# Second RWKV layer: the inverses of the last head pairs' triangles made in steps between the scan's chunks, and y of both directions kept on its half of the partitions

## The chip, the cores and the metric

The kernel is one program on one core of a Trainium2 chip. The metric is the device time of one execution in microseconds (us). A core has five engines that run side by side and meet through semaphores: PE (TensorE, matrix products; its weight loads are shown as PEld), DVE (VectorE), ACT (ScalarE), POOL (GpSimd) and SP (SyncE, which here issues DMA transfers). Each takes its own instructions strictly in the order of the program; that order is fixed when the kernel is built.

## What is computed

The program is a whole model step; the change lies in its second RWKV-7 layer, whose core is a recurrence over the tokens, in two directions and 16 heads of 64:

```python
def rwkv7_scan(state0, r, decay, k_dir, v, kk, a, emit):
    ...
    def step(S, inp):
        w_t, k_t, v_t, kk_t, a_t = inp[:5]
        s_kk = jnp.einsum('nbhvk,nbhk->nbhv', S, kk_t)
        S = S * w_t[..., None, :] - s_kk[..., :, None] * (kk_t * a_t)[..., None, :] + v_t[..., :, None] * k_t[..., None, :]
        y_t = jnp.einsum('nbhvk,nbhk->nbhv', S, inp[5]) if emit else None
        return S, y_t

    s_final, ys = lax.scan(step, state0, seqs)
    ...
    ys = jnp.moveaxis(ys, 0, 2)
    y = ys[0] + jnp.flip(ys[1], axis=1)
    return s_final, y.reshape(bsz, length, RWKV_WIDTH)

def rwkv7_output(y, r, k_dir, v, z, r_k, ln_gain, ln_bias, w_out):
    ...
    yn = ((yh - mean) * lax.rsqrt(var + RWKV_LN_EPS)).reshape(y.shape) * ln_gain + ln_bias
    ...
    return (out * jax.nn.silu(z)) @ w_out
```

The kernel doesn't go token by token. It cuts the 768 tokens (256 of context, 512 latent) into 12 chunks of 64. Within a chunk the recurrence becomes matrix products, if the inverse of a 64x64 triangle is at hand for each chunk, head and direction. These triangle inverses are what the change moves.

## The kernel before

**Stages.** `_rwkv_features` (L651) goes over eight head pairs `hp`. For each it runs the projections, which stand as filler among the rest, and twice `direction` (one for each direction: the decays, `th` at L767, the scaled keys `bk` at L783 and L785, `ra` at L784 and L807/L809, and the triangles, which go to memory as `MD`). Then `_rwkv_scan` (L928) runs the chunks, `_rwkv_out` (L1078) normalises what they give, and the products with `w_out` follow.

**A triangle's inverse** is made in two steps. `_rwkv_diagonal` (L870) inverts the 32x32 blocks on the diagonal, 128 of them at a time, one on each partition. The 768 blocks of all pairs make six such lots, i = 0 to 5, which this text calls **blocks one to six**; lots 0 to 2 hold pairs 0 to 3, lots 3 to 5 pairs 4 to 7. Each is one load of `lm` from `MD`, two clears of `lw` on POOL, then 31 rounds of two DVE instructions, a product into `tm` (L881) and a sum into `lw` (L883), each needing the one before it; one ACT copy turns `lw` round, and the results are stored as `TL` and `TV`. `_rwkv_inverse` (L899) fills in the remaining 32x32 quarter for one pair: loads of `tt` and `v1`, then eight groups of 12 small matmuls (four into `pq`, four into `pw`, taken in turn, each evicted by ACT; the trace has two records for each matmul), then a store to `TD`, from where the scan loads it as `td`.

**When.** Blocks are made at the end of the turns hp = 1, 2, 3, 5, 6, 7; the inverse of a pair is started a turn later (`LAG`). Pairs 6 and 7 remain after the last turn; `inverses(9)` is returned as the generator `late`, which the scan advances once per chunk, with `issue_after` on the chunk's last matmul (L1052). The tiles `lm`, `lw` and `tm` lie in pool `rd`, which is closed before the scan's pools are opened on the same memory.

**The scan.** There are two chains, q = 0 for the even pairs and q = 1 for the odd ones, each of 4 pairs x 3 segments x 4 chunks, 48 chunks; chain 1 is two steps behind. `chunk` (L989) is issued with high priority. In it the matmuls L998 and L1000 give `x` (evicted at L1002 as `xs`), those of L1005 give `z` (evicted into `zv` at L1006 on ACT and L1007 on DVE), L1010 gives what is added to the state `S` (L1014, two DVE instructions), and the last ones give `y`. Both directions are worked at once: direction 0 on one half of the 128 partitions, direction 1 on the other. `prepare` (L953) makes ready the next segment while a segment runs: DMA loads of `kb`, `ar`, `td`, `zv` on SP's queue, the scaled keys `ks` on POOL (L974) with four transposes on PE (L976) and an eviction on ACT (L977), and the masked products `pgm` on PE (L983) and `aq` on DVE (L985). The first use of a set of buffers also clears the halves that are not loaded (L946, L948, L949, on POOL).

**y.** Before, `ys` is a tile of 64 partitions; each chunk's `py` (128x128) is evicted in two pieces of 64x128, direction 1's moved to partitions 0 to 63, by DVE for odd chunks (L1022) and ACT for even ones (L1024). `_rwkv_out` adds both directions in one DVE sum (L1102), the second read backwards.

**The order** of each engine's instructions isn't written out by hand. A scheduler sets it at build time from the code's order, priorities (`high_priority`) and `issue_after`.

## Time and profile before

| | |
|---|---|
| median of 3 runs | 4413.97 us (4413.07 to 4424.48) |
| profiled execution, its own time | 4423.36 us |
| its span | 4421.6 us |
| busy share of the span: PE, PEld, DVE, ACT, POOL | 91, 75, 62, 40, 34% |
| granted clock, mean | 0.944 |
| last feature stage of this layer | to about 2763 us |
| the scan's first `pgm` / first chunk | 2789.15 / 2842.11 us |
| the scan's last chunk | about 3254 us |

The profile is one execution, its times counted from the start of its span. The busy shares are means over many stages with different limits; for a change in one stage one reads that stretch. A row of the timeline gives in square brackets how long the engine was idle before the instruction, and which instruction or transfer ended the idle time ("<-DMA lm<-md": a transfer into `lm`). The granted clock is TensorE's as a share of its full 2.4 GHz.

### The profile page before, as it was taken

The page shows a single profiled execution, that of the slowest core. Times are in us where ns is not written, and L with a number is a line of the kernel's source. Part 1 is how long each engine was busy: PE and PEld are TensorE (multiplying, and loading weights), DVE is VectorE, ACT ScalarE, POOL GpSimd, SP SyncE. Part 2 cuts the span into 40 slices and gives each one's busy share as a digit, 9 for nine tenths or more (in the row PEclk, how much of TensorE's full clock was granted, in tenths as well). Part 3 has the DMA queues.
Part 4 walks back from the last instruction along what each step waited for, and adds up shares of the span by engine and source line. Part 5 has one row for each costly group of instructions (what it writes and reads, how often), then busy time and mean ns, then how long its engine had stood idle before and what let it go on. Part 6 is the DMA issues. An engine that isn't in the chain of part 4 may idle for free.

```text
span 4421.6 us, 67663 instructions
## 1 busy us (share of the span) xinstructions
PE 4026.0 (91%) x26396; PEld 3301.2 (75%) x26396; DVE 2741.8 (62%) x4409; ACT 1750.0 (40%) x3351; POOL 1513.2 (34%) x1046
## 2 busy tenths in 40 slices
PE   5888999988989999999988889588889999999999
PEld 3766767756766779888977777476668888887987
DVE  6455476776697874446676777555655466764443
ACT  4444454532232334224344445233323355543321
POOL 4332144453444441223335534335521222211221
PEclk7999999988999999999998989699989999999999
DMA  5123121235445563224534776654422311132232
GB/s 188 59 66 96 51 81 53 82 109 195 136 143 156 171 188 106 91 91 156 174 121 159 230 220 184 155 131 119 113 68 76 112 51 49 50 99 92 86 96 86
DMA packets 345551, 518.46 MB, mean 117 GB/s; under 512 B 114424, under 2 KB 217464, under 8 KB 343696
## 3 DMA queue, kind: packets, MB, share of 16 engines
q1 hardware_dynamic: 339040, 502.08, 37.4%
q10 hardware_dynamic: 6192, 12.06, 0.8%
q8 instruction: 208, 3.41, 0.3%
q14 instruction: 111, 0.91, 0.1%
HBM read 425.86 MB, written 88.19 MB: 116 GB/s over the span
## 4 chain that ended last, share of the span: by engine, by line
PE 58%; DVE 15%; DMA 7%; issue 4%; ACT 3%; POOL 2%; SPq 1%; DVEq 0%; ACTq 0%; POOLq 0%
DVE macc L127 3%; PE pz L102 3%; PE pz L103 3%; PE pz L101 3%; PE po L102 2%; DMA mraw<-mw 2%; PE po L101 2%; PE po L103 2%; PE pgm L983 2%; PE pu L101 2%; PE pu L103 2%; PE pu L102 2%; PE pv L101 2%; PE pv L102 2%; PE pv L103 2%
## 5 line engine op out<-in xcount | busy, mean ns | idle before, releaser
L93 POOL TENSOR_TENSOR wlo<-raw,whi 128x1024 fp32r<-128x1024 f32 (+2 forms) x254 | 570.8, 2248 | 1339.5 <-ACT whi L91 968.2
L91 ACT ACTIVATE whi<-raw 128x1024 fp32r<-128x1024 f32 (+3 forms) x399 | 383.4, 962 | 710.3 <-PE pz L102 132.2
L95 DVE TENSOR_TENSOR wlo<-raw,whi 128x1024 fp32r<-128x1024 f32 (+3 forms) x278 | 351.6, 1266 | 288.2 <-ACT whi L91 281.8
L127 DVE SCALAR_TENSOR_TENSOR macc<-mraw,conds,macc 128x1024 f32<-128x1024 f32 x168 | 268.8, 1615 | 37.7 <-DMA mraw<-mw 37.4
L103 PE MATMUL pu<-xh,wlo 128*128 128x512 f32 x608 | 243.6, 401 | 10.5 <-DVE wlo L95 6.6
L101 PE MATMUL pu<-xh,whi 128*128 128x512 f32 x608 | 241.2, 401 | 4.3 <-DVE fu L2054 3.0
L102 PE MATMUL pu<-xl,whi 128*128 128x512 f32 x608 | 242.3, 399 | 0.0
L89 DVE CAST whi<-raw 128x1024 fp32r<-128x1024 f32 (+2 forms) x133 | 98.1, 738 | 151.6 <-PE pz L102 46.6
L226 POOL TENSOR_TENSOR rsr<-rsv,mhalf 128x4 f32<-128x4 f32 (+3 forms) x56 | 77.8, 1391 | 276.1 <-DVE rsv L224 258.5
L102 PE MATMUL pz<-xl,whi 128*128 128x512 f32 x384 | 150.0, 391 | 0.0
L103 PEld LDWEIGHTS pu<-xh,wlo 128*128 128x128 f32 x608 | 116.2, 191 | 39.5 <-DVE wlo L95 7.5
L101 PE MATMUL pv<-whi,xh 128*128 128x256 f32 x512 | 139.0, 283 | 6.9 <-ACT whi L91 6.1
L983 PE MATMUL pgm<-ar,kb 128*128 128x256 f32 x384 | 122.1, 442 | 24.8 <-DMA ar<-fe 15.7
L102 PE MATMUL pv<-wlo,xh 128*128 128x256 f32 x512 | 142.4, 282 | 0.0
L101 PEld LDWEIGHTS pu<-xh,whi 128*128 128x128 f32 x608 | 116.4, 192 | 33.5 <-issue 4.1
L103 PE MATMUL pv<-whi,xl 128*128 128x256 f32 x512 | 140.3, 282 | 0.5 <-DVE xl L258 0.5
L102 PEld LDWEIGHTS pu<-xl,whi 128*128 128x128 f32 x608 | 116.4, 191 | 27.5 <-issue 0.3
L102 PE MATMUL po<-slo,whi 128*128 128x512 f32 (+1 forms) x384 | 136.1, 357 | 0.0
L103 PE MATMUL po<-shi,wlo 128*128 128x512 f32 (+1 forms) x384 | 135.4, 357 | 0.0
L101 PE MATMUL po<-shi,whi 128*128 128x512 f32 (+1 forms) x384 | 133.9, 364 | 0.5 <-ACT shi L111 0.5
L334 POOL TENSOR_TENSOR u<-u,z 128x512 f32<-128x512 f32 (+1 forms) x48 | 58.4, 1217 | 165.2 <-DVE z L325 165.2
L101 PE MATMUL pl<-xlh,whi 128*128 128x512 f32 x208 | 93.1, 451 | 13.2 <-DVE rp L1479 10.2
(747 smaller groups left out, 12948.7 us busy)
## 6 DMA issues: line engine op xcount, KB each, us to landing
mraw<-mw SPq DMA_DIRECT2D x128, 512.0 KB
raw<-G_wuz SPq DMA_DIRECT2D x96, 512.0 KB
raw<-G_wv SPq DMA_DIRECT2D x48, 512.0 KB
raw<-G_wout SPq DMA_DIRECT2D x48, 512.0 KB
raw<-F_w_up SPq DMA_DIRECT2D x44, 512.0 KB
raw<-R_w_in SPq DMA_DIRECT2D x70, 256.0 KB
raw<-S_w_xbc SPq DMA_DIRECT2D x24, 512.0 KB
fe<-ra SPq DMA_DIRECT2D x16, 768.0 KB
```

What stands on the lines that cost most here:

```text
L89: nc.vector.tensor_copy(hi, raw)
L91: nc.scalar.activation(hi, raw, AF.Copy)
L93: nc.gpsimd.tensor_tensor(lo, raw, hi.bitcast(F32), op=ALU.subtract)
L95: nc.vector.tensor_tensor(lo, raw, hi.bitcast(F32), op=ALU.subtract)
L101: nc.tensor.matmul(ps, a[0], b[0], start=start, stop=False)
L102: nc.tensor.matmul(ps, a[0], b[1], start=False, stop=False)
L103: return nc.tensor.matmul(ps, a[1], b[0], start=False, stop=stop)
L127: nc.vector.scalar_tensor_tensor(acc, raw, c[:, kt:kt + 1], acc, op0=ALU.mult, op1=ALU.add)
L226: nc.gpsimd.tensor_tensor(r, v, self.mhalf[:, :n], op=ALU.pow)
L334: nc.gpsimd.tensor_tensor(u, u, z, op=ALU.mult)
L983: nc.tensor.matmul(pgm[:, d], kb[:, i, d, :], ar[:, i, d], start=True, stop=True)
```

## The change

1. `_rwkv_diagonal` becomes a generator that yields after every fourth round and at its end.
2. In the features stage only blocks one to three are made, in turns 1 to 3, now in pool `ri` (`ipool`), which stays open through the scan. The inverses of pairs 0 to 3 are made there as before.
3. What the features return as `late` is now a chain: blocks four and five, the inverses of pairs 4 and 5, block six, two empty steps, the inverses of pairs 6 and 7. The scan advances it as before, once per chunk.
4. `ys` gets 128 partitions, and a chunk's `py` is evicted by one 128x128 instruction in place of two, by DVE for odd chunks and ACT for even ones. `_rwkv_out` first copies direction 1's half, backwards, to partitions 0 to 63 on ACT (28 copies, 20 of them of 64x512), then adds on DVE.

```diff
--- before.py
+++ after.py
@@ -827,7 +827,13 @@
         while done and done[0][0] <= hp:
             p = done.pop(0)[1]
-            yield from _rwkv_inverse(K, ipool, mts[p], TL[p], TV[p], tt, TD[p])
+            yield from inverse(p)
+
+    def inverse(p):
+        return _rwkv_inverse(K, ipool, mts[p], TL[p], TV[p], tt, TD[p])
+
+    def diagonal(i):
+        return _rwkv_diagonal(K, ipool, MD, TL, TV, i)
 
     mts, done = {}, []
     filler = fill()
@@ -854,12 +860,12 @@
             d1 = direction(hp, 1, k, r, nkk, l2)
             mts[hp], aks, _ = zip(d0, d1)
             bonus(hp, r, aks)
-        g = hp % 4
-        if g:
-            _rwkv_diagonal(K, rd, MD, TL, TV, hp // 4 * 3 + g - 1)
-            done.extend((hp + LAG, p) for p in ((hp - 1,) if g < 3 else (hp - 1, hp)))
+        if 0 < hp < 4:
+            for _ in diagonal(hp - 1):
+                pass
+            done.extend((hp + LAG, p) for p in ((hp - 1,) if hp < 3 else (hp - 1, hp)))
     c_f.close()
-    return inverses(9)
+    return chain(diagonal(3), diagonal(4), inverse(4), inverse(5), diagonal(5), (None,) * 2, inverse(6), inverse(7))
 
 
 NTEMP = 4
@@ -881,6 +887,8 @@
         nc.vector.tensor_tensor(tv, lm[:, 0:u, u:u + 1].to_broadcast([P, u, 32 - u]),
                                 lw[:, u:u + 1, u:32].to_broadcast([P, u, 32 - u]), op=ALU.mult)
         nc.vector.tensor_tensor(lw[:, 0:u, u:32], lw[:, 0:u, u:32], tv, op=ALU.add)
+        if u % 4 == 0:
+            yield
     lt = lm
     nc.scalar.activation(lt.rearrange("l t s -> l s t"), lw, AF.Copy)
 
@@ -894,6 +902,7 @@
             m = min(48 - u, n)
             nc.scalar.dma_start(TV[hp][u:u + m], lt[l0:l0 + m])
         u0 += n
+    yield
 
 
 def _rwkv_inverse(K, pool, mts, tl, tv, tt, td):
@@ -1017,11 +1026,10 @@
                 nc.tensor.matmul(py[ZR[d], h, :], ar[:, i, d, h, 0:64], S[:, d, :], start=True, stop=False)
             for d in range(2):
                 mm = nc.tensor.matmul(py[ZR[d], h, :], aq[:, d, h, 0:64], zv[:, i, d, h, :], start=False, stop=True)
-        for d in range(2):
-            if i % 2:
-                nc.vector.tensor_copy(y[:, i, d], py[ZR[d]])
-            else:
-                nc.scalar.activation(y[:, i, d], py[ZR[d]], AF.Copy)
+        if i % 2:
+            nc.vector.tensor_copy(y[:, i], py)
+        else:
+            nc.scalar.activation(y[:, i], py, AF.Copy)
         return mm, S2
 
 
@@ -1043,7 +1051,7 @@
                 if seg == 0:
                     states[q] = pool.tile([P, 2, CH], F32, tag="S", bufs=4, name=K.nm("S"))
                     nc.gpsimd.memset(states[q], 0.0)
-                ys[q] = pool.tile([64, 4, 2, 2, CH], F32, tag="ys", bufs=6, name=K.nm("ys"))
+                ys[q] = pool.tile([P, 4, 2, CH], F32, tag="ys", bufs=6, name=K.nm("ys"))
                 if n < 11:
                     ahead[q] = prepare(n + 1, q, *todo[q][n + 1], tiles)
             with K.tc.high_priority():
@@ -1098,8 +1107,8 @@
         nc.sync.dma_start(vo[:, 2 * j:2 * (j + n)].rearrange("p (i h) v -> p i (h v)", h=2),
                           VT[0][ts, hp * P:(hp + 1) * P].rearrange("(i p) f -> p i f", p=CH))
         nc.sync.dma_start(z[:, at[-1][1]], ZD[hp][:, ts])
-        back = y1[R, ::-1, 1]
-        nc.vector.tensor_tensor(y[:, js], y0[R, i:i + n, 0], back[:, i:i + n], op=ALU.add)
+        nc.scalar.activation(y[:, js], y1[V, ::-1][:, i:i + n], AF.Copy)
+        nc.vector.tensor_tensor(y[:, js], y0[R, i:i + n], y[:, js], op=ALU.add)
         j += n
     nc.vector.reduce_sum(mn, y3, axis=AX.X)
     nc.vector.tensor_scalar(mn, mn, 1.0 / CH, None, op0=ALU.mult)
```

Where the code stands says little of where the instructions go, since the scheduler orders them. Three places on DVE show it. The names are the buffers' with a number each; `lm`, `lw` and `tm` are those of a diagonal block. Line numbers after are 4 to 9 higher (L887 and L889 are L881 and L883 of before, L994 is L985, L1016 is L1007, L1023 is L1014).

DVE at the end of the features stage, before the change: the last two rounds of block four, then the last feature work of the last-but-one direction and of the last one (`th_24314`, `bk_24340`, `ra_24339`); `zo` is a projection's tile.

```order
L883 TENSOR_TENSOR lw_23275<-lw_23275,tm_23365 128x2x30
L881 TENSOR_TENSOR tm_23368<-lm_23273,lw_23275 128x31
L784 TENSOR_TENSOR ra_24149<-nkk_23454,e_4663_24135 128x12x64
L809 TENSOR_TENSOR ra_24149<-r_23456,e_4663_24135 128x12x64
L883 TENSOR_TENSOR lw_23275<-lw_23275,tm_23368 128x31
L783 SCALAR_TENSOR_TENSOR bk_24150<-th_24140,nkk_23454 128x12x64
L722 SCALAR_TENSOR_TENSOR zo_24056<-zo_24056,pc_24057 128x256
L785 SCALAR_TENSOR_TENSOR bk_24150<-bk_24150,th_24124 128x12x64
L722 SCALAR_TENSOR_TENSOR zo_24056<-zo_24056,pl_24058 128x512
L783 SCALAR_TENSOR_TENSOR bk_24340<-th_24330,nkk_23454 128x4x64
L767 SCALAR_TENSOR_TENSOR th_24314<-rmask,th_24314 128x768
L783 SCALAR_TENSOR_TENSOR bk_24340<-th_24330,nkk_23454 128x8x64
```

DVE at the same place after the change, from the row behind block four's last one: the same feature work, and in it the first rounds of block five (`lm_24722`); the last row is the beginning of the last direction's `bk`.

```order
L767 SCALAR_TENSOR_TENSOR th_23800<-rmask,th_23800 128x768
L784 TENSOR_TENSOR ra_23825<-nkk_23351,e_4588_23811 128x12x64
L809 TENSOR_TENSOR ra_23825<-r_23353,e_4588_23811 128x12x64
L783 SCALAR_TENSOR_TENSOR bk_23826<-th_23816,nkk_23351 128x12x64
L722 SCALAR_TENSOR_TENSOR zo_23732<-zo_23732,pc_23733 128x256
L785 SCALAR_TENSOR_TENSOR bk_23826<-bk_23826,th_23800 128x12x64
L722 SCALAR_TENSOR_TENSOR zo_23732<-zo_23732,pl_23734 128x512
L887 TENSOR_TENSOR tm_24727<-lm_24722,lw_24724 128x31
L889 TENSOR_TENSOR lw_24724<-lw_24724,tm_24727 128x31
L887 TENSOR_TENSOR tm_24730<-lm_24722,lw_24724 128x60
L889 TENSOR_TENSOR lw_24724<-lw_24724,tm_24730 128x30x2
L783 SCALAR_TENSOR_TENSOR bk_23898<-th_23888,nkk_23351 128x4x64
```

Block four's end has moved ahead of the last-but-one direction's `ra` and `bk`, and block five's beginning stands ahead of the last direction's `bk`, where before all of block five stood behind it.

DVE where the scan begins, before: the last round of block six, then the first products `aq` (the first chunks' operands), and the first chunk's `zv` and `S`.

```order
L881 TENSOR_TENSOR tm_24502<-lm_24407,lw_24409 128x31
L883 TENSOR_TENSOR lw_24409<-lw_24409,tm_24502 128x31
L985 TENSOR_TENSOR aq_24583<-pgm_24580,r_rmask 128x512
L985 TENSOR_TENSOR aq_24588<-pgm_24585,r_rmask 128x512
L985 TENSOR_TENSOR aq_24593<-pgm_24590,r_rmask 128x512
L985 TENSOR_TENSOR aq_24598<-pgm_24595,r_rmask 128x512
L1007 COPY zv_24544<-c_4765_24660 64x128
L1014 SCALAR_TENSOR_TENSOR S_24682<-S_24657,gam,c_4765_24660 128x64 x2
```

The same place after: the first four `aq` and the first chunk's `zv`, with rounds of block five around them.

```order
L994 TENSOR_TENSOR aq_24039<-pgm_24036,r_rmask 128x512
L889 TENSOR_TENSOR lw_24724<-lw_24724,tm_24990 128x12x20
L994 TENSOR_TENSOR aq_24044<-pgm_24041,r_rmask 128x512
L887 TENSOR_TENSOR tm_25044<-lm_24722,lw_24724 128x231
L889 TENSOR_TENSOR lw_24724<-lw_24724,tm_25044 128x11x21
L887 TENSOR_TENSOR tm_25047<-lm_24722,lw_24724 128x220
L994 TENSOR_TENSOR aq_24049<-pgm_24046,r_rmask 128x512
L889 TENSOR_TENSOR lw_24724<-lw_24724,tm_25047 128x10x22
L887 TENSOR_TENSOR tm_25050<-lm_24722,lw_24724 128x207
L994 TENSOR_TENSOR aq_24054<-pgm_24051,r_rmask 128x512
L889 TENSOR_TENSOR lw_24724<-lw_24724,tm_25050 128x9x23
L1016 COPY zv_24000<-c_4648_24116 64x128
```

Before, blocks five and six stand wholly ahead of the first `aq`. After, the first `aq` stands ahead of block five's last 11 rounds, and block six is not there.

DVE some chunks later, before: only `aq` of the next segments and the chunks' `zv` and `S`.

```order
L1007 COPY zv_24544<-c_4784_24786 64x128
L1014 SCALAR_TENSOR_TENSOR S_24808<-S_24738,gam,c_4784_24786 128x64 x2
L985 TENSOR_TENSOR aq_25182<-pgm_25179,r_rmask 128x512
L1007 COPY zv_24601<-c_4795_24848 64x128
L1007 COPY zv_24544<-c_4805_24918 64x128
L1014 SCALAR_TENSOR_TENSOR S_24870<-S_24845,gam,c_4795_24848 128x64 x2
```

After, the same kind of chunk work with rounds of block six (`lm_26337`) in it.

```order
L887 TENSOR_TENSOR tm_26404<-lm_26337,lw_26339 128x175
L1023 SCALAR_TENSOR_TENSOR S_24533<-S_24386,gam,c_4731_24511 128x64 x2
L994 TENSOR_TENSOR aq_24798<-pgm_24795,r_rmask 128x512
L889 TENSOR_TENSOR lw_26339<-lw_26339,tm_26404 128x25x7
L887 TENSOR_TENSOR tm_26407<-lm_26337,lw_26339 128x192
L889 TENSOR_TENSOR lw_26339<-lw_26339,tm_26407 128x24x8
L887 TENSOR_TENSOR tm_26455<-lm_26337,lw_26339 128x207
L1016 COPY zv_24057<-c_4740_24568 64x128
L889 TENSOR_TENSOR lw_26339<-lw_26339,tm_26455 128x23x9
L887 TENSOR_TENSOR tm_26458<-lm_26337,lw_26339 128x220
L889 TENSOR_TENSOR lw_26339<-lw_26339,tm_26458 128x22x10
L887 TENSOR_TENSOR tm_26461<-lm_26337,lw_26339 128x231
```

Block six's rounds now stand between the chunks' `zv`, `S` and the next segments' `aq`, some two to four instructions between two of the chunks' own. On PE, the groups of pairs 4 and 5, which stood ahead of the first chunk, now stand between chunks 18 and 42 of the 96, and those of pairs 6 and 7 between chunks 44 and 65.

## Rows read from the trace of the kernel before

**Rows 1.** Busy time by stretch: us, each engine, granted clock, DMA share, GB/s.
```profile
core 0: us, PE busy (x) PEld busy (x) DVE busy (x) ACT busy (x) POOL busy (x), PEclk, DMA share, GB/s
2477.00:2763.00 286.00, 257.34 (x2360) 214.62 (x2362) 230.18 (x383) 144.95 (x270) 120.72 (x110) 0.87 0.69 202
2763.00:2842.00 79.00, 33.49 (x481) 29.33 (x476) 53.94 (x136) 17.36 (x31) 18.49 (x24) 0.55 0.69 156
2842.00:2966.00 124.00, 113.73 (x1760) 91.90 (x1760) 55.11 (x149) 40.34 (x114) 45.28 (x50) 0.90 0.50 125
2966.00:3254.00 288.00, 247.30 (x3919) 195.56 (x3916) 179.02 (x487) 94.82 (x287) 129.33 (x125) 0.95 0.41 110
```

**Rows 2.** Timeline of the hole: start us, us, engine, line, operation [idle before].
```profile
2762.89 1.77 DVE L783 SCALAR_TENSOR_TENSOR bk<-th,nkk 128x256 f32<-128x256 f32 x1 [0.95 <-ACT th L754]
...
2772.27 0.21 DVE L881 TENSOR_TENSOR tm<-lm,lw 128x31 f32<-128x31 f32 x1 [1.66 <-DMA lm<-md]
...
2813.49 0.20 DVE L881 TENSOR_TENSOR tm<-lm,lw 128x31 f32<-128x31 f32 x1 [13.59 <-DMA lm<-md]
...
2841.36 1.29 DVE L985 TENSOR_TENSOR aq<-pgm,r_rmask 128x512 f32<-128x512 f32 x2 [4.46 <-DMA tv<-lm]
...
2849.34 0.47 DVE L1014 SCALAR_TENSOR_TENSOR S<-S,gam,c 128x64 f32<-128x64 f32 x2 [0.71 <-PE c L1010]
...
2784.06 1.93 POOL L946 MEMSET ar<- 64x1024 f32 x2 [8.65 <-DMA md<-mt]
...
2785.93 0.52 POOL L948 MEMSET zv<- 64x512 f32 x1
...
2841.40 2.04 POOL L974 TENSOR_TENSOR ks<-kb,gam 128x512 f32<-128x512 f32 x2 [32.31 <-DMA tv<-lm]
...
2789.15 2.07 PE L983 MATMUL pgm<-ar,kb 128*128 128x256 f32 x4
...
2842.11 0.48 PE L998 MATMUL c<-zv,aq 128*64 128x64 f32 x4 [14.85 <-DMA tt<-tl]
...
2847.14 0.66 PE L976 MATMUL pb<-ident,ks 128*128 128x128 f32 x4
...
2848.77 0.45 PE L1010 MATMUL c<-zv,bk 128*64 128x64 f32 x8 [0.58 <-DVE zv L1007]
...
2847.84 0.60 ACT L977 ACTIVATE bk<-pb 128x512 f32<-128x512 f32 x1 [0.30 <-PE pb L976]
```

**Rows 3.** Waits, 2780 to 2860 us: us in total, times, longest.
```profile
POOL ks L974 <- DMA tv<-lm: 32.3, 1, 32.3
```

**Rows 4.** Block four (its own DVE time, then all engines) and block six (all engines).
```profile
2703.00:2757.00 54.00, 31.07 (x62) 0.91 0.53 146
...
2703.00:2757.00 54.00, 50.43 (x516) 42.72 (x516) 50.41 (x86) 25.13 (x48) 23.97 (x21) 0.91 0.53 146
...
2813.00:2837.00 24.00, 10.38 (x168) 9.44 (x168) 21.25 (x62) 3.67 (x9) 0.00 (x0) 0.50 0.26 50
```

**Rows 5.** Inverse groups in the scan: tile pq, then tile pw.
```profile
2842.00:2966.00 124.00, 8.60 (x192) 7.05 (x192) 3.86 (x8) 0.90 0.50 125
...
2842.00:2966.00 124.00, 10.07 (x192) 8.02 (x192) 3.83 (x8) 0.90 0.50 125
```

**Rows 6.** Chunks by stretch, counted by their xs evictions on ACT (x).
```profile
2873.00:2966.00 93.00, 5.34 (x20) 0.93 0.47 116
2966.00:3254.00 288.00, 19.13 (x72) 0.95 0.41 110
```

**Rows 7.** Evictions of y, squares: ns min/median/max, first and last start; forms.
```profile
L1024 ACT ACTIVATE ys<-c x96: 254/273/276, 2849.7 to 3252.7; 64x128 f32<-64x128 f32 x96
...
L1108 ACT ACTIVATE ysq<-y x26: 416/617/631, 2885.5 to 3267.8; 64x512 f32<-64x512 f32 x20, 64x384 f32<-64x384 f32 x4, 64x256 f32<-64x256 f32 x2
```

**Rows 8.** Waits of PE in the scan, 3003 to 3253 us.
```profile
PE pgm L983 <- DMA ar<-fe: 9.8, 7, 2.9
```

**Rows 9.** A load of the inverses in the chain of waits: start us, us.
```profile
2918.90 5.43 DMA tt<-tl
```

## The prediction

> **What bounds the kernel now.** The shares of the whole span help little here, since the change touches one stage; I read that stage in this order. First the busy times by stretch [rows 1]. In the features stage (2477 to 2763 us) PE is busy for 257 of 286 us. From 2763 to 2842 it is busy for 33 of 79 us, at a granted clock of 0.55, that is about the lower of its two levels (1.2 and 2.4 GHz). In the scan (2842 to 3254) it is busy for 361 of 412 us. So there is a hole of 79 us between features and scan.
>
> Then the timeline of that hole [rows 2]. The last feature work that the scan's operands need, the `bk` of the last direction, starts at 2762.89. The scan's buffers are cleared from 2784.06, its first `pgm` matmul runs at 2789.15. But the first chunk's matmul comes at 2842.11. In between DVE runs the fifth block of diagonal inverses, 62 instructions from 2772.27; then it waits 13.59 us for the load of the sixth block's `lm`, and starts that at 2813.49; block five had ended at 2799.90. The first `aq` comes at 2841.36, after an idle 4.46, so block six ended at 2836.90. The waits name what follows [rows 3]: POOL's first `ks` waits 32.3 us for the transfer `tv<-lm`, the last reader of `lm`. `lm` and `lw` lie in pool `rd`, which closes before the scan's pools open on the same memory, so the scan can't write `ks` or `aq` before the last diagonal block has left it; DVE's order says the same, with all of block six ahead of the first `aq`.
>
> In the scan itself the waits of PE are short: in 250 us the longest entry is 9.8 us, for a load of `ar` [rows 8]. PE is the bound there, so what is added to PE counts nearly in full.
>
> **The change part by part.** *Start of the scan.* Blocks four to six now lie in `ri`, which stays open, so the memory wait of 32.3 us goes. The order shows that blocks four and five stay where they were; block five now begins earlier, its first four instructions ahead of `bk` (L783) of the last direction, and its tail lies between the scan's first `aq`; block six moves behind chunk 3. What is late next? Two things. (a) Block five's first instruction waits for `lm`, in DVE's order now ahead of L783. Today L783 starts at 2762.89 and `lm` is there for the instruction at 2772.27 [rows 2], after a wait for that very transfer: if `lm` comes no earlier, the last feature work slips by 9.4 us; if it is there in time, by nothing. The store of `MD` that it reads is issued by the last-but-one direction, whose work moves up a little behind block four's earlier end (the first place of DVE's order), so I take 5. Twelve of block five's instructions now stand ahead of L785, each between 0.21 us (the first, [rows 2]) and 0.34 (the mean of block six, 21.25/62, [rows 4]): 3 us. Slip: 8 us, between 3 and 12.4. (b) POOL's clears: from 2784.06 on there are now three pairs of `ar` (1.93 us a pair) and nine of `zv` and `td` (0.52 each) ahead of `ks`: 10.5 us. So `ks` starts at 2784.06 + 8 + 10.5 = 2802.6; then one `ks` 1.02, the transposes about 0.7, their eviction 0.6, and the chunk's `S` matmuls 0.45: the first `S` update starts at about 2806, where today it starts at 2849.34 [rows 2]. **Start: 43 us earlier** (39 to 48 by the slip; 30 if a memory wait of the new layout, which no row shows, holds it further). PE's clock gives nothing: it falls in a hole of 40 us as it did in one of 79.
>
> *Inverses of pairs 4 and 5.* They cost nothing today: their 16 groups of small matmuls lie in the hole. In the scan the price is to be seen from pairs 6 and 7, which run there already. Two bounds: the 16 groups have 8.60 + 10.07 = 18.7 us of PE there [rows 5]; and the 20 chunks from 2873 to 2966, with 15 of the groups, take 93 us, where the 72 chunks after them take 288, or 4.0 each [rows 6]: 93 - 80 = 13 us, 14 for 16 groups. **+16.5 us** (14 to 18.7), between the two since neither row is nearer.
>
> *Block six in the scan.* Alone it takes 21.25 us, and POOL is then at 0.00; block four takes 31.07 us with POOL busy for 23.97 of 54 [rows 4]. In the scan POOL is busy for 129 of 288 us [rows 1], much as there, so 31 us is the size. DVE has room (179 of 288 us busy [rows 1]), and spread over some 18 chunks the block adds 1.7 us of DVE to each. It costs only where a block instruction stands ahead of `zv` or `S` when that is ready. 0 if always hidden, 31 if never. Each chunk has two such places; a wait of half an instruction of 0.5 us (31/62) at each gives 18 x 2 x 0.25 = 9, less a little that PE hides: **+7 us**, nearer to 0 since PE, not DVE, is the bound.
>
> The Trainium skill (GPSIMD Engine Reference, section 1, Specifications) says that GpSimd's SBUF interfaces are shared with VectorE, with contention for DVE instructions that take two inputs from SBUF. A block's instructions are of that kind, so by this rule moving block six beside a busy POOL is a loss in itself; the trace agrees in size, 21.25 us beside an idle POOL and 31.07 beside a busy one, but block four also ran with more DMA and PE work beside it. Without the rule the block would cost 18 x 2 x 0.17 = 6 in place of 9, and the sum would be 2 us lower.
>
> *SP.* The two inverses bring their loads (`tt`, `v`) and a store (`td`) between the segments' loads on SP's in-order queue. A `tt` takes 5.43 us [rows 9], and I estimate the same for the store of the same tile. Behind them stand `ar`, `zv` and `td` loads of the next segment, for which PE waits. In the stretch that has two inverses today PE lost little to it, so **+2 us** (0 to 22, below).
>
> *y.* 96 evictions of 64x128 on each of ACT and DVE (273 ns on ACT [rows 7], about as much on DVE) become 48 of 128x128 on each, at the price of `xs`, which has that size: 19.13/72 = 0.27 us [rows 6]. That is 13 us less on each, none of it on PE. 28 copies on ACT are new, most of 64x512, at the 0.617 us of the square of that size [rows 7]: 16 us. All of it lies beside PE; on the path only at the end, where the last sums wait for one copy more: **+0.5 us**.
>
> Sum: -43 + 16.5 + 7 + 2 + 0.5 = **-17 us**. The profiled execution took 4423.36 us (span 4421.6), 9.4 above the median of 4413.97; of its own time that gives 4406, and of the median **4397 us**.
>
> **Rivals.**
> 1. *Everything hides.* `lm` is in time (start -48), inverses at 14, block six in DVE's idle time, y's lighter evictions pay for the rest: -34, **4380 us**. For it: DVE idles for 109 of 288 us in the scan [rows 1]. Against: the slip.
> 2. *DVE takes the bound over from PE* while block six runs, each of its instructions in the way of a chunk's `zv` or `S`: +31 instead of 7, sum +7, **4421 us**, no change. For it: in the windows of blocks four and six DVE is busy for 50.41 of 54 and 21.25 of 24 us, so a block leaves little room there [rows 4]. Against: one chunk in five only.
> 3. *SP becomes late.* At each of the four inverses a store and a load (2 x 5.43 = 10.9 us) hold the next segment's loads; four times is 44: -43 + 18.7 + 7 + 44 = +27, **4441 us**, slower. It decides from the point where `ar` lands behind the `pgm` that reads it; PE waits for it already, 9.8 us in 7 places [rows 8], so there is no slack. Against: two inverses in the scan today show no such hold.
> 4. *The start doesn't move as far*: a wait on memory or `lm` leaves 15 of the 43 us: -15 + 26 = +11, **4425 us**.
>
> **How the numbers follow.** Forecast 0.50 (4397, its own range 4386 to 4408), rival 1 0.17, rival 2 0.16, rival 3 0.10, rival 4 0.07. 0.3% is 13 us, about what a measurement of this kernel can tell from no change. Faster by more than that (below 4401): all of rival 1 and 0.7 of the forecast, 0.52. Within: the rest of the forecast, rival 2 and half of rival 4, 0.34. Slower: rival 3 and the rest, 0.14. The range holds the forecast and rivals 1, 2 and most of 4: 4374 to 4428.
>
> **What would show it.** The first `S` update near 2806 us, POOL's `ks` without the 32 us wait: start right. If DVE waits 9 us or more for `lm` ahead of L783, the slip was too small. 32 inverse groups in the scan at about 1.1 us each, the scan some 26 us longer from its first chunk to its last. Block six with 30 us of DVE; PE waits for `zv` and `S` of under 10 us in its stretch. More than 20 us of PE waits for `ar` or `td` would be rival 3. The forecast is wrong if the first chunk is still behind 2830, or the scan grows by more than 40 us.

## The result: 0.988 of the time before, three times the forecast gain

The changed kernel takes 4363.75 us (median of 4 runs, 4357.2 to 4369.79) where the kernel before takes 4415.93 beside it: a ratio of 0.9878, 95% interval 0.9863 to 0.9894, or -52 us. The direction of the forecast was right. Its size, -17 us, was not: the time lies below the range of 4374 to 4428. A second set of runs of the changed kernel gave 0.9866 (0.9851 to 0.9881).

In the profiled executions the span goes from 4421.6 to 4363.5 us. I cut it at three marks of the trace: the start of the last `bk` row (L783 on DVE), the first and the last eviction `xs` of the 96 chunks (on ACT). From the last `bk` to the first `xs`, the hole, it is 81.0 us before (2766.25 to 2847.26) and 30.2 after (2764.63 to 2794.84). From the first to the last `xs`, the scan, it is 406.2 before and 403.8 after. So -50.8 us came from the hole and -2.4 from the scan, which has 16 more groups of inverse matmuls and block six in it; the remaining -4.9 lies ahead of these marks (-1.6) and behind them (-3.3). These are two single executions, 58.1 us apart, where the medians are 52 apart.

The busy times by stretch of the changed kernel, to be read against [rows 1] (us, each engine, granted clock, DMA share, GB/s):

```profile
2477.00:2763.00 286.00, 253.96 (x2370) 212.74 (x2368) 231.24 (x383) 147.97 (x275) 121.62 (x112) 0.89 0.72 207
2763.00:2795.00 32.00, 12.93 (x105) 10.05 (x106) 28.82 (x54) 3.98 (x8) 19.73 (x27) 0.57 0.75 192
2795.00:2915.00 120.00, 108.91 (x1684) 86.48 (x1684) 90.75 (x239) 43.33 (x112) 51.14 (x54) 0.97 0.53 143
2915.00:3199.00 284.00, 257.34 (x4348) 208.98 (x4346) 162.12 (x430) 102.96 (x284) 122.22 (x117) 0.95 0.48 123
```

The features stage is as it was. The stretch in which PE is mostly idle has shrunk from 79 to 32 us, and DVE is now busy in it for 28.82 of 32 us, mostly with block five. PE's share in what follows has risen: 257.34 of 284 us where it was 247.30 of 288.

The timeline of the changed kernel in the hole, against [rows 2] (start us, us, engine, line, operation, idle before):

```profile
2762.42 1.04 DVE L887 TENSOR_TENSOR tm<-lm,lw 128x31 f32<-128x31 f32 x1 [2.05 <-DMA lm<-md]
...
2764.13 0.42 DVE L783 SCALAR_TENSOR_TENSOR bk<-th,nkk 128x256 f32<-128x256 f32 x1
...
2775.08 0.95 DVE L785 SCALAR_TENSOR_TENSOR bk<-bk,th 128x768 f32<-128x768 f32 x1
...
2781.97 3.89 POOL L955 MEMSET ar<- 64x1024 f32 x4
...
2787.32 4.20 PE L992 MATMUL pgm<-ar,kb 128*128 128x256 f32 x8 [5.67 <-DMA ar<-fe]
...
2790.70 0.69 DVE L994 TENSOR_TENSOR aq<-pgm,r_rmask 128x512 f32<-128x512 f32 x1 [2.02 <-PE pgm L992]
...
2792.20 1.03 POOL L983 TENSOR_TENSOR ks<-kb,gam 128x512 f32<-128x512 f32 x1
...
2801.32 0.47 DVE L1023 SCALAR_TENSOR_TENSOR S<-S,gam,c 128x64 f32<-128x64 f32 x2
```

Block five finds its `lm` at 2762.42, after 2.05 us of waiting, and the last direction's `bk` starts at 2764.13 (before: 2762.89). The last step of that `bk`, L785 at 2775.08, has twelve instructions of block five ahead of it. In the kernel before it is this row:

```profile
2769.13 1.48 DVE L785 SCALAR_TENSOR_TENSOR bk<-bk,th 128x768 f32<-128x768 f32 x1
```

So by L785 the feature work slips by 6 us, near the 8 that I had taken. But the scan's start does not slip with it: POOL's clears begin at 2781.97, where before they began at 2784.06 and I had them 8 us later. POOL's first `ks` runs between them at 2792.20 with no wait, and the first `aq` waits for PE's `pgm`, not for memory. The first `S` comes at 2801.32; I had it at 2806, and before it was at 2849.34.

The inverse groups in the scan (tile `pq`, then `pw`; PE, PEld and ACT), block six's own DVE time and all engines beside it, and the longest wait of PE in the scan (us, times, longest), in the changed kernel and then in the kernel before:

```profile
2795.00:3199.00 404.00, 17.15 (x384) 14.09 (x384) 7.70 (x16) 0.96 0.49 129
...
2795.00:3199.00 404.00, 19.34 (x384) 14.92 (x384) 7.61 (x16) 0.96 0.49 129
...
2824.00:2876.00 52.00, 26.95 (x62) 1.00 0.42 115
...
2824.00:2876.00 52.00, 45.48 (x747) 35.80 (x747) 49.42 (x134) 16.44 (x48) 18.44 (x18) 1.00 0.42 115
...
PE pgm L992 <- DMA ar<-fe: 10.0, 8, 2.4
...
PE pgm L983 <- DMA ar<-fe: 15.7, 12, 2.9
```

The 32 groups take 17.15 + 19.34 = 36.5 us of PE, 1.14 each, as forecast (1.1). Block six takes 26.95 us of DVE beside a POOL that is busy for 18.44 of 52 us, between the 21.25 and 31.07 of [rows 4]. SP is not late: PE waits 10.0 us for `ar` in the whole scan, where before it waited 15.7. All the work is there, at the size expected, and yet the scan is no longer. That is what the experiments had to explain.

### The profile page after: what moved, and what is told of

Read it like the earlier page. It is cut to its first block, busy times and chain, and to the rows that moved or that the text cites. A ratio compares the mean times of both kernels' runs of the same rounds, so it can differ in the third digit from the quotient of the medians.

```text
span 4363.5 us, 67568 instructions
## 1 busy us (share of the span) xinstructions
PE 4007.8 (92%) x26396; PEld 3288.7 (75%) x26396; DVE 2739.3 (63%) x4361; ACT 1751.1 (40%) x3331; POOL 1507.5 (35%) x1046
## 5 line engine op out<-in xcount | busy, mean ns | idle before, releaser
L127 DVE SCALAR_TENSOR_TENSOR macc<-mraw,conds,macc 128x1024 f32<-128x1024 f32 x168 | 272.0, 1634 | 36.8 <-DMA mraw<-mw 36.5
L102 PEld LDWEIGHTS pu<-xl,whi 128*128 128x128 f32 x608 | 116.0, 191 | 29.1 <-DVE xl L258 1.8
L992 PE MATMUL pgm<-ar,kb 128*128 128x256 f32 x384 | 116.8, 427 | 18.9 <-DMA ar<-fe 15.7
```

The lines of the kernel that those rows point to most:

```text
L102: nc.tensor.matmul(ps, a[0], b[1], start=False, stop=False)
L127: nc.vector.scalar_tensor_tensor(acc, raw, c[:, kt:kt + 1], acc, op0=ALU.mult, op1=ALU.add)
L992: nc.tensor.matmul(pgm[:, d], kb[:, i, d, :], ar[:, i, d], start=True, stop=True)
```

## The experiments

Two theories stood at the beginning. **A:** the start of the scan gave the whole gain, and the work added to the scan hides in time in which the engines wait. **B:** the added work costs the 24 us of the prediction, and the lighter evictions of y gave them back. All ratios below are to the kernel before, run on the same chip beside them, with their 95% interval. "Hole" and "scan" are the two lengths defined above, in the one profiled execution of each, and "clock" is the granted clock from the first to the last `xs`.

| kernel | ratio (interval) | hole | scan | clock |
|---|---|---|---|---|
| before | 1 | 81.0 | 406.2 | 0.94 |
| changed | 0.9878 (0.9863 to 0.9894) | 30.2 | 403.8 | 0.96 |
| changed, again | 0.9866 (0.9851 to 0.9881) | 29.5 | 409.1 | 0.95 |
| y_only | 0.9906 (0.9889 to 0.9922) | 33.7 | 409.9 | 0.94 |
| y_and_pool | 0.9905 (0.9890 to 0.9920) | 35.3 | 409.8 | 0.93 |
| y_padded | 0.9960 (0.9948 to 0.9973) | 82.7 | 379.7 | 0.98 |
| y_padded_two | 0.9966 (0.9954 to 0.9978) | 82.9 | 392.2 | 0.95 |
| ys_three | 0.9956 (0.9944 to 0.9969) | 33.9 | 433.4 | 0.92 |
| before_swap | 0.9971 (0.9960 to 0.9983) | 82.4 | 393.3 | 0.95 |
| before_zv | 0.9971 (0.9960 to 0.9981) | 82.6 | 387.9 | 0.96 |
| no_inv45 | 0.9872 (0.9856 to 0.9887) | 31.6 | 396.0 | 0.95 |
| no_inv4567 | 0.9830 (0.9816 to 0.9843) | 29.1 | 383.5 | 0.96 |
| no_block6 | 0.9895 (0.9876 to 0.9914) | 29.0 | 421.7 | 0.91 |
| block6_small | 0.9905 (0.9887 to 0.9922) | 29.1 | 422.3 | 0.92 |
| after_two | 0.9913 (0.9898 to 0.9927) | 29.3 | 418.2 | 0.95 |
| td_on_act | 0.9897 (0.9881 to 0.9913) | 29.4 | 407.9 | 0.95 |
| after_swap | 0.9895 (0.9881 to 0.9908) | 29.3 | 418.2 | 0.94 |
| after_zv | 0.9882 (0.9866 to 0.9897) | 30.3 | 413.3 | 0.93 |

### What freed the start

First one part of the change alone, y in its new form, in the kernel before:

```diff
-        for d in range(2):
-            if i % 2:
-                nc.vector.tensor_copy(y[:, i, d], py[ZR[d]])
...
+        if i % 2:
+            nc.vector.tensor_copy(y[:, i], py)
...
-                ys[q] = pool.tile([64, 4, 2, 2, CH], F32, tag="ys", bufs=6, name=K.nm("ys"))
+                ys[q] = pool.tile([P, 4, 2, CH], F32, tag="ys", bufs=6, name=K.nm("ys"))
```

> The kernel before with the y change alone (one 128x128 eviction per chunk, the ACT copy ahead of the sum); blocks and inverses as before. Theory A (the start of the scan gave the whole gain, and the work added to the scan hid in engines' idle time): within 4 us of before, the scan 406 us from its first to its last chunk as before. Rival B (the added work cost the 24 us that the prediction has, and the lighter evictions of y shorten every chunk and gave them back): 15 to 25 us faster than before, with the scan 15 to 25 us shorter.

It gave 0.9906, -41 us, most of the whole gain. Neither theory had that: A had no difference, and B a shorter scan, but the scan is 409.9 us long. It is the hole that is shorter, 33.7 us. The blocks still lie in pool `rd` in this kernel. So the new y alone is enough to free the start, without the move of the blocks to `ri`. The last `bk` (DVE) and the first `xs` (ACT) in this kernel's timeline:

```profile
2764.91 0.66 DVE L783 SCALAR_TENSOR_TENSOR bk<-th,nkk 128x512 f32<-128x512 f32 x1
...
2798.61 0.28 ACT L1002 ACTIVATE xs<-c 128x128 f32<-128x128 f32 x1 [5.79 <-DMA td<-tt]
```

Much of the late work then runs among the chunks although no call was moved. Block six begins at 2820.73 (first row) and ends at 2859.85, and 12 of the 16 `pq` evictions on ACT, so 24 of the 32 inverse groups, come behind 2799 (second row):

```profile
2820.73 0.20 DVE L881 TENSOR_TENSOR tm<-lm,lw 128x31 f32<-128x31 f32 x1
...
2799.00:3209.00 410.00, 12.36 (x288) 10.36 (x288) 5.79 (x12) 0.94 0.50 125
```

Then the pool was changed as well, `_rwkv_diagonal(K, ipool, ...)` in place of `rd`, with all calls where they were:

> The kernel before with the y change and all six diagonal blocks in the pool that stays open, nothing moved in the code: DVE's order comes out as in the changed kernel (the first aq inside block five, block six among the chunks), but the inverses of pairs 4 and 5 stay ahead of the first chunk on PE. Theory A: if the memory wait alone held the start, this gets most of the 52 us, 4365 to 4375. Rival (PE's order holds the start too, since the first chunk stands behind groups that need block five, which ends near 2809, and their loads): the first chunk near 2825 to 2830, only 15 to 25 us faster than before, near 4395.

0.9905, as with y alone; with the new y in place the pool adds nothing. The pool without the new y was not run, so whether it would free the start by itself is not shown. The rival missed too: the hole is 35.3 us. Only pair 4's groups run in it (PE's last of them starts at 2778.46); pair 5's come from 2811.05 on, among the first chunks.

An old `ys` tile takes 4 KB on each of its partitions, the new one 2 KB, and there are six: 12 KB. Whether this memory is the cause was asked from both sides. The new form, with the tile padded to its old size:

```diff
-                ys[q] = pool.tile([P, 4, 2, CH], F32, tag="ys", bufs=6, name=K.nm("ys"))
+                ys[q] = pool.tile([P, 8, 2, CH], F32, tag="ys", bufs=6, name=K.nm("ys"))[:, 0:4]
```

> The kernel before with the y change, but the tile of ys padded to its former 4 KB per partition, so that the scan's pools lie where they lay before. Theory M (the y change works by the 12 KB that it frees: the scan's ks and aq no longer lie on the memory of the last diagonal blocks): the start of the scan goes back, 80 us between the last bk and the first chunk, POOL's ks waits over 30 us again, and the time is within 6 us of before. Rival E (the lighter evictions and the sum's form gave the 42 us): as fast as with the y change alone, 4375 to 4382.

And the old form, with three buffers (`bufs=6` to `bufs=3`) in the kernel before:

> The kernel before with 3 buffers of ys in place of 6 and nothing else: the same 12 KB are free, y as before. Theory M: the first chunk comes some 34 us after the last bk, not 81, and the time is 35 to 45 us under before, less what waits for a free ys cost later. Rival E: no faster than before, or slower by those waits.

The hole says memory in both: 82.7 us with the padding, 33.9 with three buffers. The padded kernel's longest wait of POOL from 2780 to 2860 us (us, times, longest) is that of [rows 3]; then the last `bk` and the first `xs` with three buffers:

```profile
POOL ks L974 <- DMA tv<-lm: 32.8, 1, 32.8
```

```profile
2770.80 0.66 DVE L783 SCALAR_TENSOR_TENSOR bk<-th,nkk 128x512 f32<-128x512 f32 x1
...
2804.75 0.28 ACT L1002 ACTIVATE xs<-c 128x128 f32<-128x128 f32 x1 [6.05 <-DMA ar<-fe]
```

So this much is shown: with 12 KB less in `ys`, whatever the form of y, the wait of 32 us for the memory of the last diagonal block goes. The total time did not do what theory M said, though. The padded kernel is at 0.9960, not at 1; and with three buffers the scan takes 433.4 us, so 0.9956 and not 0.991. The padded kernel's scan is 26 us shorter than that of the kernel before. The waits for a free `ys` that were expected with three buffers are only 1.9 us of that long scan (us, times, longest); the rest of its length is not explained:

```profile
ACT ys L1024 <- DVE y L1102: 1.9, 3, 1.3
```

### What the moved work costs

The changed kernel with parts of the late work left out: the groups of pairs 4 and 5, those of all four pairs (in `_rwkv_inverse`, the matmuls and evictions are skipped and the yields stay), and block six:

```diff
     for u in range(31, 0, -1):
+        if i == 5:
+            if u % 4 == 0:
+                yield
+            continue
```

> The changed kernel without the 16 groups of small matmuls of pairs 4 and 5 and their evictions (left out; their loads and stores stay). Theory A (they hide in PE's idle time): 0 to 6 us faster than the changed kernel, 4358 to 4364. Rival B (the prediction's price): 14 to 19 us faster, 4345 to 4350.

> The changed kernel without the 32 groups of small matmuls of pairs 4 to 7 and their evictions (left out; loads and stores stay). Theory A (they hide in PE's idle time in the scan): at most 10 us faster than the changed kernel. Rival B (each counts in full, as the prediction has it): 28 to 37 us faster.

> The changed kernel without the 62 DVE instructions of block six (left out; its load, clears, copy and stores stay). Theory A: 0 to 3 us faster than the changed kernel, 4361 to 4364. Rival B (the prediction's price): 7 us faster, 4357; if DVE is in the way wherever it stands, up to 25.

Without 16 groups nothing is gained that can be measured (0.9872); without 32 it is 0.9830 against 0.9878 and 0.9866, that is 16 to 21 us, where the groups have 36.5 us of PE. More than A's 10 us came out, and less than B's 28. Against the changed kernel's two other orders (below) it would be 23 and 29 us, so between a fifth and somewhat over half of the groups' time hides. The scans of the kernel before, of the changed kernel and of the one without the 32 groups, first to last `xs`:

```profile
2847.26:3253.49 406.23, 355.70 (x5636) 283.50 (x5636) 231.77 (x629) 134.28 (x398) 169.49 (x166) 0.94 0.44 114
```

```profile
2794.84:3198.63 403.79, 366.04 (x6029) 295.44 (x6030) 252.71 (x668) 146.18 (x395) 173.53 (x171) 0.96 0.49 129
```

```profile
2797.07:3180.58 383.51, 328.02 (x5260) 263.20 (x5260) 251.35 (x668) 132.37 (x363) 175.70 (x172) 0.96 0.53 134
```

PE sits idle for 403.79 - 366.04 = 37.8 us in the changed kernel and for 383.51 - 328.02 = 55.5 without the groups; before, it was 406.23 - 355.70 = 50.5. Without them PE is busy for 38.0 us less, but the scan is only 20.3 us shorter: the groups fill idle time.

Block six showed no price. Without its 62 instructions the kernel is not faster but, if anything, slower, with one of the longest scans:

```profile
2790.40:3212.06 421.66, 376.44 (x6030) 305.09 (x6030) 228.11 (x609) 148.45 (x397) 175.05 (x173) 0.91 0.48 124
```

PE has no less and no more to do than in the changed kernel, but is busy for 376.44 us, at a granted clock of 0.91. The scan's length times its clock is 421.66 x 0.91 = 384 us here and 403.79 x 0.96 = 388 in the changed kernel, so by this estimate the clock makes the whole difference between the two scans; why it is lower here is not shown. The four runs of this kernel, 4363.94, 4370.97, 4379.1 and 4379.52 us, stand in the order of their granted clock over the whole program, 0.953, 0.951, 0.946 and 0.946. To keep the instructions in place I then cut them to one element each in place of leaving them out:

> The changed kernel with block six's 62 DVE instructions cut to one element each (the rest of their work left out), so that the number and the dependences of the instructions stay. DVE has some 22 us less to do among the first 20 chunks. The prediction's price: 5 to 9 us faster than the changed kernel. If block six hides: within 4 us. If, as without block six, the time goes up, the scan's time hangs more on TensorE's granted clock (0.91 over the scan without block six, 0.95 and 0.96 in the changed kernel) than on DVE's work, and the clock in this scan says so.

0.9905 and a scan of 422.3 us at 0.92: the same. So the scan does not get shorter with less work on DVE. A price of a few us, such as the 7 of the prediction, is not excluded by that, since both edits can change the scheduler's order as well, and an order alone can make such a difference, as follows.

### The order and the clock

That left the 16 us which the new form of y gives when it frees no memory. Two evictions per chunk in place of one, each on its own half, were tried in the padded kernel and in the changed one:

```diff
-        if i % 2:
-            nc.vector.tensor_copy(y[:, i], py)
+        for d in range(2):
+            if i % 2:
+                nc.vector.tensor_copy(y[ZR[d], i], py[ZR[d]])
```

> As y_padded, but each chunk's y evicted by two instructions of 64x128 again (each on its own half of the partitions). Theory C (the second eviction stands on ACT or DVE ahead of the next chunk's xs, zv or S and lengthens every chunk by some 0.2 us): 14 to 20 us slower than y_padded, so about as before (0.998 to 1.002 of it), the scan over 400 us where y_padded has 380. Rival F (the tile on 128 partitions and the new form of the sum gave the gain, not the number of evictions): as y_padded, 0.996.

> The changed kernel with two evictions of 64x128 per chunk, each on its own half: memory, blocks and inverses as in the changed kernel. Theory C: 12 to 20 us slower than the changed kernel, 0.990 to 0.992 of before. Rival F: as the changed kernel, 0.987.

The two contradict each other: no difference in the padded kernel (0.9966 against 0.9960), 15 us in the changed one (0.9913). What the scheduler does can explain it, since another eviction gives it other instructions to order. So the last four kernels keep the work and change the order: in the kernel before and in the changed one, the engines of y's evictions are changed over (`i % 2 == 0`), or those of the two `zv` evictions.

> The kernel before with the engines of y's evictions changed over (DVE takes the even chunks, ACT the odd ones): the same work, memory and counts, but the scheduler puts some 550 of DVE's instructions elsewhere. Theory O (the scan's time hangs on the order that the scheduler happens to find, by TensorE's short waits and the clock that falls after them): anywhere from 15 us faster to 15 us slower than before. Theory Y (the new form of y saves 15 us by itself): within 5 us of before.

> The kernel before with the two zv evictions of a chunk changed over between ACT and DVE: the same work, another order (some 450 of DVE's instructions elsewhere). Theory O: anywhere from 15 us faster to 15 us slower than before. Theory Y: within 5 us of before.

> The changed kernel with the engines of y's evictions changed over: the same work, another order (some 800 of DVE's instructions elsewhere). Theory O: up to 15 us from the changed kernel, and slower rather than faster, as the other variants of it were. Theory Y: within 5 us of it.

> The changed kernel with the two zv evictions of a chunk changed over between ACT and DVE: the same work, another order. Theory O: up to 15 us from the changed kernel. Theory Y: within 5 us of it.

Both variants of the kernel before are 13 us faster than it (0.9971), with intervals that exclude 1, at the same work, memory and hole. Their gain can't be told from that of the padded y (0.9960 and 0.9966). So the lighter evictions as such are not shown to give anything; the order that the scheduler found for the kernel before is a slow one, and all four edits of its scan that keep the hole (these two, y_padded and y_padded_two) are faster. The changed kernel has no such step down: its own two variants are at 0.9895 and 0.9882, its two sets of runs at 0.9878 and 0.9866, so the variants are if anything slower, by 7 us in the mean.

How waits and the clock cost time is to be seen in a stretch of the kernel before (busy times by stretch, then PE's timeline there):

```profile
2939.00:2943.00 4.00, 3.89 (x95) 3.37 (x91) 1.90 (x6) 2.04 (x6) 2.55 (x4) 1.00 1.01 236
2943.00:2947.00 4.00, 2.66 (x13) 1.71 (x13) 0.29 (x1) 0.29 (x2) 0.68 (x1) 0.65 0.49 126
2947.00:2951.00 4.00, 4.00 (x39) 3.11 (x39) 1.46 (x4) 0.27 (x1) 0.00 (x0) 0.50 0.22 66
...
2955.00:2959.00 4.00, 4.00 (x52) 2.92 (x52) 1.73 (x6) 1.86 (x4) 2.38 (x4) 1.00 0.68 194
```

```profile
2944.34 2.08 PE L983 MATMUL pgm<-ar,kb 128*128 128x256 f32 x4 [1.45 <-DMA ar<-fe]
2946.35 0.70 PE L1005 MATMUL c<-xs,td 128*64 128x64 f32 x8
2946.97 2.08 PE L983 MATMUL pgm<-ar,kb 128*128 128x256 f32 x4
...
2957.88 1.13 PE L983 MATMUL pgm<-ar,kb 128*128 128x256 f32 x4
```

PE waits 1.45 us for a load of `ar`, and the granted clock falls to its lower level (0.50 in the next stretch); four `pgm` matmuls then take 2.08 us, where at the upper level they take 1.13 (last row, in the stretch from 2955). In the two stretches from 2943 the clock is 0.65 and 0.50, so 4 x 0.35 + 4 x 0.50 = 3.4 us of full clock are missing there, more than twice the wait (an estimate from these rows). Not every such wait is followed by a fall. In the same execution, 20 us earlier, PE waited longer, and the clock stayed at 1.00:

```profile
2924.37 0.24 PE L922 MATMUL pw<-tt,v 32*32 32x32 f32 x2 [1.88 <-DMA tt<-tl]
```

```profile
2923.00:2927.00 4.00, 2.63 (x66) 2.37 (x68) 1.39 (x4) 0.82 (x3) 0.00 (x0) 1.00 0.72 205
2927.00:2931.00 4.00, 4.00 (x61) 3.27 (x62) 1.00 (x3) 1.15 (x4) 0.00 (x0) 1.00 0.11 32
```

How long PE waits in all is not what differs between the orders, though. The scans of before_swap and before_zv, first to last `xs`:

```profile
2844.71:3237.98 393.27, 341.75 (x5638) 276.85 (x5638) 232.64 (x633) 133.16 (x397) 171.15 (x167) 0.95 0.45 118
```

```profile
2859.94:3247.81 387.87, 337.64 (x5636) 273.81 (x5636) 229.06 (x630) 138.81 (x398) 171.75 (x167) 0.96 0.45 119
```

PE is idle for 51.5 and 50.2 us in them and for 50.5 in the kernel before. It is busy there for 355.70 us, 14 and 18 us more for the same matmuls. Length times (1 - clock) is 24 us in the kernel before, 20 and 16 in these two, so the clock accounts for some 5 and 9 us of it (an estimate, from clocks rounded to 0.01). The rest was not traced.

### A store on another queue

Last, a place that looked like rival 3. In the changed kernel's trace SP issues nothing from 3072 to 3079.73, then the store `td<-tt` of the last inverse, with the next segments' loads behind it, and the eight chunks from 3069 take 41 us. ACT has just written `tt`, so it could issue the store without a wait: `(nc.scalar if act else nc.sync).dma_start(td, tt)`.

> The changed kernel with the stores td<-tt of pairs 4 to 7 issued by ACT, which has just written tt, in place of SP. If SP's wait for tt holds the next segments' loads (in the changed kernel's trace the store of the last inverse is issued at 3079.73, 7 us after SP's last issue, with the loads of kb, ar and td behind it, and the eight chunks from 3069 take 41 us): the scan 5 to 10 us shorter there, 0 to 8 us faster in all. If not: no difference, or up to 2 us slower by ACT's issue time.

0.9897, not faster, and the eight chunks there still take 40.5 us. The longest wait of SP's queue from 3055 to 3100 us (us, times, longest) in the changed kernel, then in this one:

```profile
SPq L934 <- ACT tt L932: 7.3, 1, 7.3
```

```profile
SPq L970 <- PE c L1014: 12.9, 1, 12.9
```

SP's 7.3 us for `tt` are gone, but the load of `kb` behind it now waits 12.9 us for PE. The store alone was not what held the loads.

## Why the prediction was wrong

- **Where the kernel was bound, and by what: right.** The wait of 32 us for the memory of the last diagonal block held the scan's start, and it is gone. **Who takes it away: incomplete.** I gave it to `ri` alone. The 12 KB of `ys` are enough by themselves (y_padded 82.7 us, y_only 33.7), and with them `ri` adds nothing; whether `ri` would have been enough too, no run shows. I had put y down as +0.5 us of evictions and copies and had not asked what its tile does to the memory plan, though the tile's size stands in the diff. In the total this makes no difference, since both parts are in the change.
- **Start, -43 us: 5 to 8 too little.** By the first `S` it is 48.0 us earlier, and the hole is 50.8 us shorter. The slip itself was sized well (6 us by L785). The failed sentence is the one that lays it on POOL: "So `ks` starts at 2784.06 + 8 + 10.5 = 2802.6". The clears did not wait for the slipped work, so `ks` started at 2792.20, 10 us earlier; from there to the first `S` it took 9.1 us and not 3.4. Rival 1 had -48, but for another reason, `lm` in time.
- **Inverses of pairs 4 and 5, +16.5 us (14 to 18.7): too high.** Their PE time is as forecast, but only a part of it shows: 32 groups are worth 16 to 21 us against the changed kernel itself and 22 against the mean of its four ratios (below), so 8 to 11 for 16, under my lower bound; only against the slowest of its orders, 29 us, do they reach it. The failed sentence is "what is added to PE counts nearly in full": in the last scan row of [rows 1], which covers the waits that I read it from, PE is idle for 41 of 288 us, and with 38.0 us of PE's work left out the scan became 20.3 us shorter.
- **Block six, +7 us (0 to 31): no price seen.** Its 26.95 us of DVE are there; leaving them out gains nothing, though the scatter of orders is too wide to tell 0 from 7. The Trainium skill (GPSIMD Engine Reference, section 1, Specifications) states contention between GpSimd and DVE instructions with two inputs from SBUF. This size agrees with it, lying between that beside an idle and that beside a busier POOL, but no loss of time is seen to come of it here. **SP, +2 us: about 0.** PE waits 10.0 us for `ar` in the whole scan, less than the 15.7 before. Rival 3's 44 us counted all four inverses, of which the kernel before has two in its scan already; for the two new ones it would have been 22.
- **The order of the scan: no term at all, about -13 us.** The sum took the 406.2 us of the scan as what its work takes. The same work in two other orders takes 393.3 and 387.9 us, 0.9971 of the time. No such bad luck is in the changed kernel: its two sets of runs and its two other orders have a mean of 0.9880, and its own order is if anything a lucky one. Order against order, the change is worth about 40 us and not 52: 36 with the two variants of either kernel alone, 43 with all three orders of each.

So some 9 to 16 us of the 52 are luck with the order, above all the slow one of the kernel before. The rest can be laid out by the profiled executions of the two variants of before and of the four of the changed kernel (changed, again, after_swap, after_zv). Their mean holes are 82.5 and 29.8 us, their mean scans 390.6 and 411.1. So the start gives -53, and the work moved into the scan costs some 20 us by its length, or 10 to 16 as what is left of the 36 to 43, where I had 25.5. The sum thus lacked 5 to 8 us at the start, 5 to 15 in the costs and 13 for the order of the kernel before, all with the same sign. Of the four rivals none was this; "everything hides", at -34, was the nearest. The range was too narrow since its ends were built from the costs alone: the scatter that a new order brings, some 13 us here, belonged into it.

Not settled: how much of the 12 to 17 us between y_and_pool and the changed kernel comes from doing the inverses in steps. The hole is 5 us shorter, the scan's length is the same within the scatter that orders give, and 0.9905 is close to the 0.9895 and 0.9913 of the changed kernel's variants.

## What to carry to other kernels

Ask of every tile that changes its size what memory it frees or takes, and who waited for that memory: here the size of a tile that is first written in the scan decided when the scan could start. An engine that is busy for 86% of a stretch still has room for small work between its waits, so price an addition also by what the same engine's idle time can take in, and not by its busy time alone. And where a scheduler orders a stage, an edit anywhere in it draws a new order; run one or two edits that change the order and nothing else before a gain of some 0.3% is put down to a cause.

## What the runs showed of the hardware

Behind one wait of PE of 1.45 us in the scan the granted clock fell to the lower level; behind one of 1.88 us, 20 us earlier, it did not. What tells the two apart no run here shows. Over the whole scan the clock was 0.91 to 0.98 of full clock in these kernels. With less work on DVE (no_block6, block6_small) the scan was at 0.91 and 0.92 and took 18 us longer than that of the changed kernel at 0.96.

The same 62 DVE instructions took 21.25 us beside an idle POOL, 26.95 beside one that was busy for 18.44 of 52 us, and 31.07 beside one that was busy for 23.97 of 54. Other engines' work differed between the three as well.
